# A fused transformer layer on one core: T's last quarter in another buffer, the FFN's first sums and w_down's sums at other places, and the third head's split values in buffer a

## The chip, the cores and the metric

The kernel runs on one core of a Trainium2 chip. Its engines are TensorE (PE, matmuls; PEld is its weight load), VectorE (DVE), ScalarE (ACT), GpSimd (POOL) and SyncE (SP, which here only issues transfers). Each engine works through its own queue in order; semaphores tie the queues together. The metric is the device time of one execution in microseconds, as the median of several runs.

## The reference

One layer of a hybrid encoder on x of 1024 tokens by 1024 channels: token mixing, cross-attention into 256 memory tokens, and a SwiGLU FFN, each between RMS norms and with a residual.

```python
h = rms_norm(x, mix_pre_g); proj = h @ w_in          # u | q | k | v | f_logit
y_ssm = s5_mixer(u, ...)                             # 32 groups x 16 channels, scan, gelu, GLU
y_fox = forgetting_attention(q, k, v, f_logit)       # 8 heads x 64, causal, decaying bias
x = x + rms_norm(concat(rms_norm(y_ssm), rms_norm(y_fox)) @ w_out, mix_post_g)
h = rms_norm(x, xa_pre_g)
x = x + rms_norm(memory_cross_attention(h, rms_norm(mem), wq, wkv, wo), xa_post_g)   # 4 heads x 256
h = rms_norm(x, ffn_pre_g)
x = x + rms_norm((silu(h @ w_gate) * (h @ w_up)) @ w_down, ffn_post_g)              # hidden 2816
```

## The kernel before

Every large product runs as three matmuls on operands split in a high and a low part (hi·hi, hi·lo, lo·hi; `mm3`, L122 to L124). `split` makes the parts: ACT copies the source to the high part (L113), DVE subtracts it for the low part (L115). The FFN's products (L1313) and the down projection's (L1591) have a function of their own with the same three matmuls.

The program is written as Python generators that yield between small pieces of work. A framework schedules it: it gives every buffer from a pool with a fixed number of slots, and it sets the order of each engine's queue from the program's order, from priorities (`tc.high_priority`), and from when buffers come free in its own timing of the program. So a buffer in another pool, or a call at another place, moves instructions of all engines around it. The pools that matter here are `slab` (16 large buffers), the small tags of `tt` ("a" 2, "b" 2, "c" 3, "d" 1, "e" 1, "t2" 3, which the trace calls t), `whl` (3, split weights), `raw` (2, weights as loaded), psum banks g (4) and x (4), and the FFN's `ev` (13, results of products) and `op` (10, split weights).

Three places matter.

The SSM's output. `ssm` prepares the state matrices and loads three quarters of the matrix T (made earlier and kept in `T_d`; the first quarter stays on the chip in the tile called e). `ssm_out` then has two halves s_, each of four groups b; a group is four pairs of matmuls (L647 with T, L648 with the states), summed in one psum bank, and a gelu on ACT (L649). Around it PE multiplies values: `v_tiles` makes tiles of 24 matmuls (128x256), ACT evacuates each with L318 into a t2 buffer, and POOL stores it. The split q and k tiles go through t2 and buffer a as well (L291 to L300), to `qk_d`. Buffer d holds the row `rb` that L291 multiplies by.

The out projection of the token mixing. For eight tiles of tokens j (a loop over n) PE makes two halves of 12 matmuls into x banks; DVE scales and adds (L1089), ACT squares (L1091), POOL multiplies by the gain (L1093), and DVE's L1095 to L1097 finish the row into c or e. The tiles t alternate between tags a and b. After each half `step(between)` advances `first_values`, which does matmuls of the cross-attention's values with its output weights, head by head: `value_weights(h)` loads the values of head h from `kv_d`, splits them (vh, vl), loads and splits the weights `wo`, and makes four sums of six matmuls each, which ACT and DVE evacuate. Heads 0 and 1 run inside the loop, heads 2 and 3 behind it.

The FFN. Pairs of hidden tiles are computed with seven products in place of eight (Strassen and Winograd's form): `operands` makes the sums of weights on POOL (L1416) and their splits, `gate_up` the products of a step (m is 0 for gate, 1 for up), in banks that sums are taken from: u2 is the first of them (`q.add`, DVE L1334); bank 2 is written on by a later product and has to be read first. `finish_hid` multiplies gate and up, `hid_sums` makes the four sums of the hidden tiles that the down projection's seven products want (DVE L1371), and POOL stores each to `hs_d`. `wd_sums(k)` loads a quarter of w_down's pair k // 2, makes four differences on POOL (L1386) and stores them to `wt_d` (L1387). The first pair has a start of its own and is finished by `sums(0, 1, ...)`; the loop over `seq` does the other ten pairs.

Of the kernel before, what the change touches and what calls it, by code (L numbers as in the profile page):

```python
# [9 lines left out]
F32 = mybir.dt.float32  # L10
F32R = mybir.dt.float32r
# [6 lines left out]
P = 128  # L18
# [34 lines left out]
def layer(ctx: ExitStack, tc: tile.TileContext, a, out):  # L53
# [15 lines left out]
    def slab(shape, dt=F32R):  # L69
        return slabp.tile(shape, dt, name="slab", tag="slab")  # L70
# [126 lines left out]
    def tt(tag, shape=None, dt=F32):  # L197
        return t4.tile(shape or [P, S], dt, name=tag, tag=tag, bufs=BUFS[tag])

    def t2t(shape, dt=F32):  # L200
        return tt("t2", shape, dt)
# [160 lines left out]
    def ssm():  # L362
# [20 lines left out]
        er, th, n, sn, sh, cs = cols[3:9]  # L383
# [55 lines left out]
        full = [P, NP, L, 16]  # L439
# [15 lines left out]
        for q in range(0, NP, 2):  # L455
# [4 lines left out]
            m = mi[q // 8][:, (2 * q) % 16:(2 * q) % 16 + 4, :]  # L460
# [16 lines left out]
        for b in range(8):  # L477
# [5 lines left out]
            for ri in range(2):  # L483
                for g2 in range(2):
                    o = V[ri][g2 * 64:g2 * 64 + 64, 2 * b:2 * b + 2]
                    i = ps[ri * 64:ri * 64 + 64, :, g2]
# [86 lines left out]
        tq = tt("e", [P, 8, P])  # L573
# [22 lines left out]
        for b in range(1, 4):  # L596
            n = 4 if b < 3 else 3
# [14 lines left out]
        for hf in range(2):  # L612
# [8 lines left out]
            for ri in range(2):  # L621
# [6 lines left out]
                for g2 in range(2):  # L628
                    act.activation(out=Sv[ri * 64:ri * 64 + 64, :, g2, 1:8], in_=t_[g2 * 64:g2 * 64 + 64], func=AF.Copy)
                yield  # L630
        full = [None] + [slab([P, 16, P], F32) for _ in range(2)]
        T = [[tq, full[1][:, 0:8]], [full[2][:, 0:8], full[2][:, 8:16]]]
        for hf in range(2):
            for b in range(2):
                if hf + b:
# [272 lines left out]
    with tc.high_priority(offset=boost):  # L908
# [18 lines left out]
        ws = [u_load(0)]  # L927
# [112 lines left out]
    for i in range(4):  # L1040
        hl = slab([P, 2, D])
        w = hl[:, 1].bitcast(F32)
# [4 lines left out]
    VW = {}  # L1047

    def value_weights(h):
        vh, vl = t2t([P, 2, 256], F32R), t2t([P, 2, 256], F32R)  # L1050
        vr = vl.bitcast(F32)
        sp.dma_start(out=vr, in_=kv_d[8 + 2 * h:8 + 2 * h + 2].rearrange("d p m -> p d m"))
        with tc.high_priority(offset=boost):
            split(vh, vl, vr)
        wo_ = [load_w(a["wo"][2 * h + d], 512) for d in range(2)]
        for mt in range(2):
            VW[2 * h + mt] = slab([P, 2, D])
        for c in range(2):
            tiles = [(mt, (x_ps if h == 3 else g_ps)([P, 512])) for mt in range(2)]
            for d in range(2):  # L1060
                for mt, ps in tiles:
                    ms = slice(mt * P, mt * P + P)
                    mm3(ps, vh[:, d, ms], vl[:, d, ms], wo_[d][0][:, c], wo_[d][1][:, c], d == 0, d == 1)
                    yield
            for mt, ps in tiles:
                split(VW[2 * h + mt][:, 0, c * 512:c * 512 + 512], VW[2 * h + mt][:, 1, c * 512:c * 512 + 512], ps)

    def first_values():
        for h in range(2):
            yield from value_weights(h)  # L1070

    between = first_values()
    kept = {}
# [235 lines left out]
    def product(ps, w, name, first):  # L1309
        (wh, wl), (bh, bl) = w, hB[name]  # L1310
        for k in range(4):
            for n, (x, y) in enumerate(((wh, bh), (wh, bl), (wl, bh))):
                pe.matmul(ps, x[:, k], y[:, k], start=first and k + n == 0, stop=k == 3 and n == 2,  # L1313
                          skip_group_check=not first)
# [48 lines left out]
    def hid_sums(i):  # L1363

        a11, a12, a21, a22 = hid.pop((0, 0)), hid.pop((1, 0)), hid.pop((0, 1)), hid.pop((1, 1))
        t = {}
        for name, x, y, fn in (("S3", a11, a21, ALU.subtract), ("S1", a21, a22, ALU.add),
                               ("S2", "S1", a11, ALU.subtract), ("S4", a12, "S2", ALU.subtract)):
            t[name] = ev()
            x, y = (t[v] if isinstance(v, str) else v for v in (x, y))  # L1370
            dve.tensor_tensor(out=t[name], in0=x, in1=y, op=fn)  # L1371
            hid_store(i, name, t[name])
# [55 lines left out]
        o["S1"] = op(s1)  # L1428
        return o

    def gate_up(i, m, w, q):
        q.p1(w["11"])
        p1 = q.keep(1)
        product(q.bank(4), w["S4"], "22", True)
        product(q.bank(3), w["S3"], "T3", True)
        p7 = q.keep(3)
        q.p2(w["12"])
        product(q.bank(2), w["S2"], "T2", True)
        u2 = q.add(2, p1)
        product(q.bank(3), w["22"], "T4", False)  # L1440
        product(q.bank(2), w["S1"], "T1", False)
        sums(i, m, q, p1, p7, u2, q.b[1])

    def sums(i, m, q, p1, p7, u2, c11):
        c21 = q.add(3, u2, False)
        u4 = q.add(2, p1, False)
        dve.tensor_tensor(out=p7, in0=u4, in1=p7, op=ALU.add)
        c12 = q.add(4, u4, False)
        c = {(0, 0): c11, (0, 1): c12, (1, 0): c21, (1, 1): p7}
        if m == 0:  # L1450
            for k, t in c.items():
                hid[k] = ev() if k == (0, 0) else t
                act.activation(out=hid[k], in_=t, func=AF.Silu)
        else:
            for (f, t), u in c.items():
                finish_hid(i, f, t, u)
            hid_sums(i)

    seq = [(i, m) for i in range(1, NPAIR) for m in range(2)]
    ws = {}  # L1460
# [6 lines left out]
    w = operands(0, 1, dve)  # L1467
# [15 lines left out]
    product(first.bank(3), w["22"], "T4", False)  # L1483
    product(first.bank(2), w["S1"], "T1", False)
    sums(0, 1, first, p1, p7, u2, c11)
    wd_sums(1)
    for n, (i, m) in enumerate(seq):
        if n + 1 < len(seq):
            ws[seq[n + 1]] = operands(*seq[n + 1])
        gate_up(i, m, ws.pop((i, m)), Products(i, m))  # L1490
        wd_sums(n + 2)


    fst.close()
# [168 lines left out]
```

## Time and profile before

| | before |
|---|---|
| median of 3 runs | 1402.24 us (1399.69 to 1403.91) |
| the profiled execution | 1403.55 us |
| its span, first to last instruction | 1401.8 us |
| mean granted clock of TensorE | 0.996 |
| PE busy | 1373.7 us |
| DVE, ACT, POOL busy | 973.7, 646.2, 377.3 us |
| transfers | 242.03 MB, mean 173 GB/s |

A row of a timeline reads: start, duration, engine, line, operation, result and sources, shape, count; in brackets the engine's idle time before it and what ended it. A row of the waits reads: what waited, what it waited for, total, times, longest. A row of stretches (A:B) gives busy time and count of PE, PEld, DVE, ACT and POOL, then the granted clock (1.00 is full), the share of the DMA engines and GB/s. Durations of matmuls overlap: one of 512 columns shows 0.39 us, but starts come 0.227 us apart.

### The profile page before, as it was taken

How to read it: one execution, taken by the hardware profiler on the slowest of the kernel's cores; microseconds unless marked ns; L12 is line 12 of the kernel's file. 1: busy time of each engine (PE TensorE's matmuls, PEld its weight loads, DVE VectorE, ACT ScalarE, POOL GpSimd, SP SyncE). 2: the span in 40 equal slices, each digit the busy share in tenths (PEclk: the TensorE clock that was granted, in tenths of full speed). 3: DMA queues.
4: the chain of work that ended last, by engine and by line, in shares of the span. 5: the costliest groups of instructions: out<-in, count | busy, mean ns of one | idle time of the engine just before them, and what ended most of it. 6: DMA issues, size and time to landing. Idle time of an engine off the chain costs nothing.

```text
span 1401.8 us, 19885 instructions
## 1 busy us (share of the span) xinstructions
PE 1373.7 (98%) x7149; PEld 1144.9 (82%) x7149; DVE 973.7 (69%) x1740; ACT 646.2 (46%) x1262; POOL 377.3 (27%) x430
## 2 busy tenths in 40 slices
PE   9999999999999999999999999999999999999997
PEld 7889888879978777888888778888888888888886
DVE  7959954858667678445567998787777676655566
ACT  7373345866456547433344533333333334544441
POOL 0011110001111142001111466687666651000021
PEclk9999999999999999999999999999999999999999
DMA  6435765358662865035366354555444447965544
GB/s 218 141 105 165 216 222 139 83 155 252 184 194 83 222 194 186 0 105 169 131 219 233 135 180 157 189 188 173 160 141 163 153 151 245 355 195 195 180 166 165
DMA packets 104626, 242.03 MB, mean 173 GB/s; under 512 B 11528, under 2 KB 40200, under 8 KB 104336
## 3 DMA queue, kind: packets, MB, share of 16 engines
q1 hardware_dynamic: 86000, 178.86, 40.8%
q0 software_dynamic: 18528, 61.91, 12.4%
q8 instruction: 56, 0.92, 0.3%
q14 instruction: 42, 0.34, 0.1%
HBM read 172.05 MB, written 79.43 MB: 179 GB/s over the span
## 4 chain that ended last, share of the span: by engine, by line
PE 57%; DVE 2%; issue 1%; DMA 1%; POOL 0%; ACT 0%; DVEq 0%; SPq 0%; POOLq 0%; ACTq 0%
PE x L1313 15%; PE g L1313 12%; PE x L1591 7%; PE g L1591 7%; PE g L124 2%; PE g L122 2%; PE g L123 2%; PE x L122 2%; PE x L123 2%; PE x L124 2%; PE g L1109 1%; DVE op L115 1%; PE g L1220 0%; DVE ev L1371 0%; DMA slab<-in_w_gate 0%
## 5 line engine op out<-in xcount | busy, mean ns | idle before, releaser
L1313 PE MATMUL x<-slab,op 128*128 128x512 f32 x984 | 233.4, 389 | 0.0
L1313 PEld LDWEIGHTS x<-slab,op 128*128 128x128 f32 x984 | 184.7, 188 | 38.7 <-DVE op L115 0.5
L1313 PE MATMUL g<-slab,op 128*128 128x512 f32 x756 | 182.2, 390 | 2.3 <-DVE ev L1334 2.0
L115 DVE TENSOR_TENSOR slab<-slab 128x1024 fp32r<-128x1024 f32 (+2 forms) x96 | 115.0, 1208 | 82.9 <-ACT slab L113 81.2
L1313 PEld LDWEIGHTS g<-slab,op 128*128 128x128 f32 x756 | 141.6, 188 | 32.9 <-DVE ev L1334 2.4
L122 PE MATMUL g<-slab,whl 128*128 128x512 f32 (+1 forms) x416 | 151.7, 365 | 0.8 <-ACT slab L487 0.4
L123 PE MATMUL g<-slab,whl 128*128 128x512 f32 (+1 forms) x416 | 148.4, 357 | 0.0
L124 PE MATMUL g<-slab,whl 128*128 128x512 f32 (+1 forms) x416 | 148.4, 357 | 0.0
L113 ACT ACTIVATE slab<-slab 128x1024 fp32r<-128x1024 f32 (+2 forms) x96 | 99.0, 1037 | 102.4 <-DMA slab<-hs_d 75.2
L1591 PE MATMUL g<-slab 128*128 128x512 f32 x462 | 126.6, 389 | 0.0
L1591 PE MATMUL x<-slab 128*128 128x512 f32 x462 | 126.6, 389 | 0.0
L115 DVE TENSOR_TENSOR op<-slab,op 128x512 fp32r<-128x512 f32 x82 | 99.4, 1222 | 11.9 <-ACT op L113 11.5
L1591 PEld LDWEIGHTS g<-slab 128*128 128x128 f32 x462 | 86.7, 188 | 18.0
L1591 PEld LDWEIGHTS x<-slab 128*128 128x128 f32 x462 | 86.7, 188 | 18.0
L1386 POOL TENSOR_TENSOR wt<-wt 128x256 f32<-128x256 f32 x88 | 85.7, 974 | 30.6 <-DMA wt<-in_w_down 27.3
L113 ACT ACTIVATE op<-ss 128x512 fp32r<-128x512 f32 x63 | 39.5, 629 | 106.7 <-PE g L1313 50.9
L122 PEld LDWEIGHTS g<-slab,whl 128*128 128x128 f32 x416 | 78.7, 189 | 12.2 <-ACT whl L113 0.6
L124 PEld LDWEIGHTS g<-slab,whl 128*128 128x128 f32 x416 | 78.5, 189 | 11.6 <-DVE whl L115 0.2
L123 PEld LDWEIGHTS g<-slab,whl 128*128 128x128 f32 x416 | 78.7, 189 | 10.6
L113 ACT ACTIVATE op<-slab 128x512 fp32r<-128x512 f32 x82 | 51.1, 627 | 78.4 <-PE x L1313 40.8
L115 DVE TENSOR_TENSOR whl<-raw,whl 128x1024 fp32r<-128x1024 f32 (+2 forms) x58 | 66.0, 1144 | 20.8 <-ACT whl L113 20.5
L1416 POOL TENSOR_TENSOR ss<-slab 128x512 f32<-128x512 f32 x40 | 60.8, 1520 | 62.7 <-DMA slab<-in_w_gate 22.2
(397 smaller groups left out, 2876.2 us busy)
## 6 DMA issues: line engine op xcount, KB each, us to landing
hs_d<-ev POOLq DMA_DIRECT2D x77, 256.0 KB, 2.6
slab<-hs_d SPq DMA_DIRECT2D x35, 512.0 KB, 3.9
slab<-in_w_up SPq DMA_DIRECT2D x22, 512.0 KB, 4.4
wt<-in_w_down SPq DMA_DIRECT2D x44, 256.0 KB, 3.3
wt_d<-wt POOLq DMA_DIRECT2D x22, 512.0 KB, 3.8
slab<-in_w_gate SPq DMA_DIRECT2D x20, 512.0 KB
slab<-wt_d SPq DMA_DIRECT2D x20, 512.0 KB, 8.6
wd_d<-in_w_down SPq DMA_DIRECT2D x33, 256.0 KB, 4.7
```

What stands on the lines that cost most here:

```text
L113: first = act.activation(out=hi, in_=src, func=AF.Copy, scale=1.0 if mul is None else mul)
L115: (lo_eng or dve).tensor_tensor(out=lo, in0=src, in1=hi.bitcast(F32), op=ALU.subtract)
L122: pe.matmul(ps, lh, rh, start=first, stop=False)
L123: pe.matmul(ps, lh, rl, start=False, stop=False)
L124: pe.matmul(ps, ll, rh, start=False, stop=last)
L1109: pe.transpose(tp[:, k], src[:, (k0 + k) * P:(k0 + k + 1) * P], ident)
L1313: pe.matmul(ps, x[:, k], y[:, k], start=first and k + n == 0, stop=k == 3 and n == 2, skip_group_check=not first)
L1386: pool.tensor_tensor(out=o, in0=x, in1=y, op=ALU.subtract)
L1416: made[0] = pool.tensor_tensor(out=o, in0=x, in1=y, op=fn)
L1591: pe.matmul(banks[n][j], xo[:, u, js], wo[:, v], start=ends[0] and k == 0, stop=ends[1] and k == 2, skip_group_check=onto is not None)
```

## The change

Four things are changed.

1. T's second and third quarters share one slab; the last quarter goes to buffer d. The SSM takes one slab less.
2. For the third head (h == 2) `value_weights` puts both parts of the split values in one tile of tag a in place of two t2 buffers; and `first_values` yields once more between the first two heads.
3. The four `hid_sums` of the first pair are not issued at the end of that pair, but in the first step of the second pair, behind its u2.
4. `wd_sums` runs one step later in the loop, with the last set behind the loop.

```diff
@@ ssm
-        full = [None] + [slab([P, 16, P], F32) for _ in range(2)]
-        T = [[tq, full[1][:, 0:8]], [full[2][:, 0:8], full[2][:, 8:16]]]
+        mid, tl = slab([P, 16, P], F32), tt("d", [P, 8, P])
+        T = [[tq, mid[:, 0:8]], [mid[:, 8:16], tl]]
@@ value_weights
-        vh, vl = t2t([P, 2, 256], F32R), t2t([P, 2, 256], F32R)
+        if h == 2:
+            both = tt("a", [P, 2, 2, 256], F32R)
+            vh, vl = both[:, 0], both[:, 1]
+        else:
+            vh, vl = t2t([P, 2, 256], F32R), t2t([P, 2, 256], F32R)
@@ first_values
-        for h in range(2):
-            yield from value_weights(h)
+        yield from value_weights(0)
+        yield
+        yield from value_weights(1)
@@ gate_up
-    def gate_up(i, m, w, q):
+    def gate_up(i, m, w, q, behind_u2=None):
...
         u2 = q.add(2, p1)
+        if behind_u2:
+            behind_u2()
         product(q.bank(3), w["22"], "T4", False)
@@ sums
-            hid_sums(i)
+            if i:
+                hid_sums(i)
@@ the loop
-    wd_sums(1)
     for n, (i, m) in enumerate(seq):
         if n + 1 < len(seq):
             ws[seq[n + 1]] = operands(*seq[n + 1])
-        gate_up(i, m, ws.pop((i, m)), Products(i, m))
-        wd_sums(n + 2)
+        gate_up(i, m, ws.pop((i, m)), Products(i, m), (lambda: hid_sums(0)) if n == 0 else None)
+        wd_sums(n + 1)
+    wd_sums(len(seq) + 1)
```

What this moves in the queues. First, the SSM's output on PE: g_2043 is the third group (b=2), g_2053 the fourth (b=3), g_1994 a value tile of which one matmul ran before the groups, g_2063 the next value tile. (Lines of the changed kernel are the same up to here.)

```order
 L648 MATMUL g_2043<-slab_1179,slab_1624 128x128
+L647 MATMUL g_2053<-slab_1951,slab_863 128x128
+L648 MATMUL g_2053<-slab_1179,slab_1624 128x128
...
 L123 MATMUL g_1994<-whl_1957,slab_267 128x256
 L124 MATMUL g_1994<-whl_1957,slab_271 128x256
...
 L124 MATMUL g_1994<-whl_1962,slab_274 128x256
-L647 MATMUL g_2053<-slab_1951,slab_863 128x128
-L648 MATMUL g_2053<-slab_1179,slab_1624 128x128
...
 L122 MATMUL g_2063<-whl_1957,slab_267 128x256
```

The eight rows of b=3 now stand ahead of the 23 remaining matmuls of the value tile. The same place on ACT, where L318 evacuates value tiles (g_1994 into t_2019) and L649 is the gelu of a group:

```order
 L318 ACTIVATE t_1991<-g,r_x 128x256
 L629 ACTIVATE slab<-b 64x8x112 x2
-L318 ACTIVATE t_2019<-g,r_x 128x256
 L649 ACT_TABLE_LOAD
 L649 ACTIVATE slab<-g 128x4x8x16 x4
+L318 ACTIVATE t_2019<-g,r_x 128x256
 L318 ACTIVATE t_2088<-g,r_x 128x256
```

The table load and the four gelus now stand ahead of that evacuation. On SP, the loads of T (L636) among those of q, k (L723), the decay rows nc_d and weights:

```order
-L636 DMA slab<-T_d 128x1024
-L723 DMA a<-qk_d 64x1024 x2
-L719 DMA b<-nc_d 128x1024
 L636 DMA slab<-T_d 128x1024 x2
+L723 DMA a<-qk_d 64x1024 x2
+L719 DMA b<-nc_d 128x1024
+L636 DMA d<-T_d 128x1024
 L159 DMA raw<-in_w_out_s 128x1024
```

The second load into the slab now comes with the first, ahead of the loads of q and k; the third goes to d. Second, the end of the out projection on DVE, before the change (the rows of a are those of n = 6, the rows of b those of n = 5 and then n = 7):

```order
L1089 SCALAR_TENSOR_TENSOR a<-x,r_f,a 128x512
L1097 SCALAR_TENSOR_TENSOR c<-b,r,c 128x1024
L1089 SCALAR_TENSOR_TENSOR a<-x,r_f,a 128x512
L115 TENSOR_TENSOR whl<-raw,whl 128x1024
L1095 TENSOR_REDUCE ss<-ss_5543 128x1
L139 TENSOR_SCALAR rsv<-ss 128x1
L1089 SCALAR_TENSOR_TENSOR b<-x,r_f,b 128x512
L141 SCALAR_TENSOR_TENSOR rst<-rsy,rsv 128x1
L145 SCALAR_TENSOR_TENSOR r<-rst,rsy 128x1
L1097 SCALAR_TENSOR_TENSOR c<-a,r,c 128x1024
L115 TENSOR_TENSOR slab<-g,slab 128x512
L1089 SCALAR_TENSOR_TENSOR b<-x,r_f,b 128x512
```

and after it, where five or so is added to each line number (L1094 is L1089, L1100 is L1095, L1102 is L1097):

```order
L1102 SCALAR_TENSOR_TENSOR c<-b,r,c 128x1024
L115 TENSOR_TENSOR a<-a 128x512
L115 TENSOR_TENSOR slab<-g,slab 128x512
L1094 SCALAR_TENSOR_TENSOR a<-x,r_f,a 128x512
L1100 TENSOR_REDUCE ss<-ss_5540 128x1
L139 TENSOR_SCALAR rsv<-ss 128x1
L141 SCALAR_TENSOR_TENSOR rst<-rsy,rsv 128x1
L145 SCALAR_TENSOR_TENSOR r<-rst,rsy 128x1
L1102 SCALAR_TENSOR_TENSOR c<-a,r,c 128x1024
L1094 SCALAR_TENSOR_TENSOR b<-x,r_f,b 128x512
L115 TENSOR_TENSOR whl<-raw,whl 128x1024
L1094 SCALAR_TENSOR_TENSOR b<-x,r_f,b 128x512
```

The low half of the third head's first weights (whl<-raw) stood ahead of the L1095 of n = 6 and now stands behind the last c<-a and an L1094 of n = 7; the low half of its values (a<-a) now stands early, while t<-t stood behind the last row shown of before. On PE the first product of the second head comes after one more half of the out projection, and with it all that follows of that head. Third, the FFN's start on DVE, before (L1371 the four sums, L1334 on g the u2 sum):

```order
L115 TENSOR_TENSOR op<-ss,op 128x512
L115 TENSOR_TENSOR op<-slab,op 128x512
L115 TENSOR_TENSOR op<-ss,op 128x512
L1371 TENSOR_TENSOR ev<-ev 128x512 x2
L115 TENSOR_TENSOR op<-slab,op 128x512
L1371 TENSOR_TENSOR ev<-ev 128x512 x2
L1334 TENSOR_TENSOR ev<-g,ev 128x512
L115 TENSOR_TENSOR op<-slab,op 128x512 x2
```

and after (L1376 the sums, L1339 the u2 sum):

```order
L1361 TENSOR_TENSOR ev<-ev 128x512
L115 TENSOR_TENSOR op<-slab,op 128x512
L115 TENSOR_TENSOR op<-ss,op 128x512
L115 TENSOR_TENSOR op<-slab,op 128x512 x2
L1339 TENSOR_TENSOR ev<-g,ev 128x512
L1376 TENSOR_TENSOR ev<-ev 128x512 x2
L115 TENSOR_TENSOR op<-slab,op 128x512
L1376 TENSOR_TENSOR ev<-ev 128x512
L1339 TENSOR_TENSOR ev<-x,ev 128x512
```

The u2 sum now stands ahead of the four sums and behind two more splits. On PE, ten matmuls of the next step's products, which stood ahead of the product that waits for u2 (the second one into bank 2), now stand behind it.

## The prediction

> **What bounds the kernel now.** I read the page's busy time of each engine first, then the list of what PE waits for, then the timelines and stretches around those waits.
>
> ```profile
> span 1401.8 us, 19885 instructions
> PE 1373.7 (98%) x7149; PEld 1144.9 (82%) x7149; DVE 973.7 (69%) x1740; ACT 646.2 (46%) x1262; POOL 377.3 (27%) x430
> ```
>
> PE is busy for 98% of the span, so the change can only win where PE idles or runs slowly; the number of matmuls stays the same. Where PE idles, the list of PE's waits tells (total, times, longest):
>
> ```profile
> PE g L647 <- ACT t L318: 3.2, 1, 3.2
> ...
> PE g L1313 <- DVE ev L1334: 2.0, 1, 2.0
> PE g L124 <- DVE t L115: 1.9, 2, 1.4
> ```
>
> L647 is the SSM's output, L1313 behind L1334 the FFN's start, L124 behind L115 the products with the split values: the diff touches these three places, and what I can win stands there; what I can lose is not bounded by the list.
>
> **The SSM's output (T's last quarter in buffer d).** The timeline of PE shows the end of the third group of products (b=2), 23 value matmuls, the wait, the fourth group (b=3) and a second wait; two rows of stretches give the granted clock (PEclk) around it:
>
> ```profile
> 193.55 0.39 PE L648 MATMUL g<-slab 128*128 128x128 f32 x2
> 193.69 0.36 PE L123 MATMUL g<-whl,slab 128*128 128x256 f32 x1
> ...
> 196.40 0.28 PE L124 MATMUL g<-whl,slab 128*128 128x256 f32 x1
> 199.85 0.70 PE L647 MATMUL g<-slab 128*128 128x128 f32 x2 [3.17 <-ACT t L318]
> ...
> 203.80 0.39 PE L122 MATMUL g<-whl,slab 128*128 128x256 f32 x1 [0.27 <-ACT slab L649]
> 193.70:197.00 3.30, 2.98 (x26) 2.78 (x24) 0.00 (x0) 0.00 (x0) 0.00 (x0) 1.00 0.92 322
> 200.00:203.50 3.50, 3.50 (x16) 3.24 (x16) 0.00 (x0) 1.45 (x2) 0.54 (x1) 0.52 1.03 419
> ```
>
> Between 193.69 and 203.80 PE does 23 value matmuls at about 0.12 us (2.98 us) and eight double rows which at full clock take 0.224 each (1.79 us, from the spacing of the b=2 rows). That is 4.8 us of work in 10.1 us. 3.17 + 0.27 is idle; about 1.9 us is the half clock, 0.52, that b=3 gets behind the idle stretch. Why b=3 waits, ACT, SP and POOL tell:
>
> ```profile
> 190.91 1.91 ACT L629 ACTIVATE slab<-b 64x896 f32<-64x896 f32 x2
> 199.32 0.47 ACT L318 ACTIVATE t<-g,r_x 128x256 f32<-128x256 f32 x1 [6.50 <-DMA qk_d<-t]
> 199.81 1.28 ACT L649 ACT_TABLE_LOAD   x1
> 203.15 2.07 ACT L649 ACTIVATE slab<-g 128x512 f32<-128x512 f32 x4 [2.05 <-PE g L647]
> 190.30 1.07 POOL L299 DMA_DIRECT2D qk_d<-t  x2 [6.38 <-ACT t L113]
> 184.11 0.33 SPq L636 DMA_DIRECT2D slab<-T_d  x1
> 187.54 1.14 SPq L723 DMA_DIRECT2D a<-qk_d  x2
> 190.24 0.80 SPq L636 DMA_DIRECT2D slab<-T_d  x2
> ```
>
> b=3 takes the psum bank of a value tile; that tile's evacuation (L318) needs a t2 buffer, and the store from it, issued at 190.30, lands nine microseconds later. With the change, b=3 stands ahead of the 23 value matmuls on PE, takes the bank of b=0, and needs b=0's gelu instead. ACT has the table load and the four gelus ahead of that L318. L629 ends at 192.82; table load 1.28, one gelu 2.07/4 = 0.52: 194.62. b=2 ends at about 193.75, so PE waits about 0.9 us, runs b=3 at full clock (1.79) and the 23 value matmuls (2.98) and is at the next value matmul at about 199.4 instead of 203.80. By then the other gelus are done, and the L318 that waits to 199.3 for its buffer holds only a tile that ends at the same moment. Gain 4.4 us. Bounds: 5.3 (no wait at all) and 2.5 (b=3 still at half clock). What pays: the second T load passes the two a<-qk_d loads on SP, 0.3 us of issue for them; nothing in PE's list waits for those. The last quarter in d waits for the last reader of d, DVE's L291, and then goes out where the x2 row stands now, 190.24; w_out_s and nc_d queue behind it there as before. It is read by the second half's products, some 20 us later. Cost nothing.
>
> The Trainium skill, "TensorE: Matmul & The Clock Gate", Part 1 (The HAM clock gate), says that an idle window of about 3.4 us halves the clock and a busy one restores it. The trace agrees for this place (3.17 us idle, then 0.52). By that rule a wait of 0.9 us costs no clock, as I took it.
>
> **The split values of the third head in buffer a, and a half step between the first two heads.** PE's waits there, and what ACT, DVE and SP do ahead of them:
>
> ```profile
> 536.12 0.50 PE L122 MATMUL g<-whl,t 128*128 128x512 f32 x1 [0.69 <-ACT t L113]
> 538.29 0.74 PE L124 MATMUL g<-whl,t 128*128 128x512 f32 x2 [0.51 <-DVE t L115]
> 531.02 1.05 ACT L113 ACTIVATE whl<-raw 128x1024 fp32r<-128x1024 f32 x1
> 532.10 1.53 DVE L115 TENSOR_TENSOR whl<-raw,whl 128x1024 fp32r<-128x1024 f32 x1
> 535.09 1.28 DVE L1097 SCALAR_TENSOR_TENSOR c<-a,r,c 128x1024 f32<-128x1024 f32 x1
> 536.89 0.74 DVE L1089 SCALAR_TENSOR_TENSOR b<-x,r_f,b 128x512 f32<-128x512 f32 x1
> 535.00:546.00 11.00, 8.81 (x41) 6.34 (x40) 10.69 (x17) 9.60 (x24) 3.66 (x2) 1.00 0.67 219
> ```
>
> The change gives the third head's values a free buffer early, so the waits of 0.69 and 0.51 for them go. The longer of the two waits of L124 in the list, 1.4, stays: DVE's order up to that split is unchanged and the same number of matmuls stands ahead of that lo product. But the half step delays the second head by 12 matmuls, and with its last product the release of the weight buffer that the third head's first weights want. On DVE the lo half of these weights moves from 532.10 to behind the last c<-a (535.09 to 536.3) and the next L1089 b (0.67 apart), so it ends at about 536.3 + 0.7 + 1.2 = 538.1 at the latest, and half a microsecond to a microsecond sooner, as the two 0.6 us splits that stood between them are gone: 537.5. PE comes to its first use at about 535.5 (536.12 less the 0.69 that it no longer waits): a new wait of about 2.0. Next late are the evacuations of the second head's last sums: DVE has another head's values (0.6) and another weight (1.2) ahead of them, and the third head's next product wants that bank: about 2 us more, where 0.51 and smaller waits stand now. DVE is full here, 10.69 of 11 us, so nothing is caught up. About 3.6 us of new waits less 1.2 us of old ones: a loss of 2.4 us. Bounds: a gain of 1.2 (the old waits go, none comes) and a loss of 4.4 (the load below).
>
> **The FFN's first sums.** DVE before PE's longest wait in this phase:
>
> ```profile
> 812.61 2.88 PE L1313 MATMUL x<-slab,op 128*128 128x512 f32 x12
> 825.23 3.70 PE L1313 MATMUL g<-slab,op 128*128 128x512 f32 x15 [2.00 <-DVE ev L1334]
> 818.21 2.92 DVE L1371 TENSOR_TENSOR ev<-ev 128x512 f32<-128x512 f32 x2
> 824.49 0.68 DVE L1334 TENSOR_TENSOR ev<-g,ev 128x512 f32<-128x512 f32 x1
> 825.09 3.89 DVE L115 TENSOR_TENSOR op<-slab,op 128x512 fp32r<-128x512 f32 x2
> ```
>
> The u2 sum (L1334) stands behind four L1371 sums (two such pairs) and one split. With the change two splits are ahead of it instead, one of the 3.89 pair among them: 818.21 + 0.6 + 2.1 (the larger share of the 3.89) + 0.6 = 821.5 in place of 825.1. But PE gains less, since ten matmuls of the next products now stand behind this wait and not ahead (12 take 2.72, the 2.88 of the x12 row less the 0.16 by which a last one outlasts its place, so ten take 2.3): it arrives at 825.23 - 2.00 - 2.3 = 820.9 and waits 0.6, or with a second slow split 1.5. Gain about 0.9, between the two; bounds 2.0 (the split takes 0.6, as most do) and -0.3. The four sums and their stores on POOL come later, into ring buffers that no PE row waits for.
>
> **w_down a step later** moves loads (SP), sums and stores (POOL, 27% busy). After the last step one set of sums is now done a step, 84 matmuls or 19 us, later:
>
> ```profile
> 1156.12 0.74 POOL L1387 DMA_DIRECT2D wt_d<-wt  x1 [0.30 <-POOL wt L1386]
> 1185.49 0.42 SPq L1512 DMA_DIRECT2D slab<-wt_d  x1
> ```
>
> 1156.12 + 19 is 1175, before even the first load from wt_d, and that load reads other pairs. The FFN between has no PE wait to win. Nothing, 0.3 either way.
>
> **Sum.** -4.4 + 2.4 - 0.9 = -2.9 us. Against the profiled execution (1403.55, of which 1401.8 is span) that is 1400.7; the median of the runs, 1402.24, lies 1.3 under it, so I say 1399.4.
>
> A second row of half clock has no such long wait in front of it:
>
> ```profile
> 278.35:281.76 3.41, 2.83 (x24) 2.55 (x24) 2.37 (x7) 2.76 (x8) 0.00 (x0) 1.00 0.62 153
> 281.76:285.18 3.42, 3.42 (x9) 2.66 (x9) 1.84 (x7) 2.39 (x4) 0.73 (x2) 0.52 0.53 146
> ```
>
> Half of 3.42 us, 1.7, is lost here, though PE was busy for 2.83 of the stretch before. Whether a loose stretch meets a window is chance, worth 1.7 us either way, for the new waits of the third head too. Read strictly, the Trainium skill (the page and part named above: a whole idle window) would not halve the clock after a stretch as busy as this; the row shows it, so the measurement decides.
>
> **Rivals.**
> First, the third head costs nothing and the FFN gives all: the evacuations are caught up because ACT has room (9.60 of 11 us) and the splits do not collide. Then -4.4 - 1.2 - 2.0 = -7.6, about 1394.6; with only one of the two, 1397. Against it: DVE's 10.69 of 11. With region one at its upper bound and half of these, faster: 0.3.
> Second, the change does not do what it says at the SSM: the gelu of b=0 comes as late as L318 did, since T's loads and 0.92 to 1.03 of the DMA engines' time still stand there, or the next value tile waits for the t2 buffer instead. Then only the loss of 2.4 and the gain of 0.9 are left, 1403.7, no difference to be measured. Against it: in this trace the first three groups ran without a wait, up to 193.55, and a gelu of b=0 needs no transfer.
> Third, slower: the load a<-kv_d. On SP it waits for DVE's e<-a and stands between two c<-in_x; ACT's split of it stands ahead of the next squares, which feed r for all that follows.
>
> ```profile
> t<-kv_d SPq DMA_DIRECT2D x4, 256.0 KB, 4.0
> 521.79 9.74 SPq L1082 DMA_DIRECT2D c<-in_x  x2
> 524.33 1.28 DVE L1097 SCALAR_TENSOR_TENSOR e<-a,r,e 128x1024 f32<-128x1024 f32 x1
> 528.43 0.20 ACT L138 ACTIVATE rsy<-rsy 128x1 f32<-128x1 f32 x1
> ```
>
> Issued at 525.6 with the 4.0 us of its kind it lands at 529.6, one microsecond after ACT is free for it, which DVE's work covers; each microsecond more holds ACT and DVE. Taking nine microseconds, like the store at 190.30, it lands at 534.6: 5 us of hold, -2.9 + 5 = +2.1, with a half clock behind it +3.8. It decides from about 11 us on, when the hold is past 2.9 + 4.2 = 7.1.
>
> **Chances.** 0.3% of the time, 4.2 us, is what a measurement can tell from no change. My forecast, between -4.2 and +1 of the median: 0.50; the first rival and region one's upper bound, past -4.2: 0.30; the second: 0.13; the third: 0.07, taken whole as slower. So faster 0.30, same 0.63, slower 0.07. The range, 1395 to 1404.5, reaches the first rival nearly to its end and the second. The likeliest case alone: 1398 to 1403.
>
> **What would show it.** Right: the row of L647 with a wait near 0.9 by L649, PEclk 1.00 there, PE's L122 at about 199.4; waits near 2 by DVE whl L115 and DVE slab L115 around 534; L1313's wait by L1334 between 0.5 and 1.5. Wrong: L647 still waiting for L318 or for T, the ACT row a<-a waiting for kv_d, or PE waits in the FFN by wt or ev.

## The result and the profile after

The changed kernel takes 1411.57 us in the median of 6 runs (1410.71 to 1419.51), the kernel before 1401.88 us in 6 runs beside it (1399.69 to 1404.71). The ratio is 1.0077, with a 95% interval of 1.0052 to 1.0102: about 9.7 us slower. I had forecast 1399.4 us and a range up to 1404.5. The prediction is wrong, in sign too.

The profiled execution of the changed kernel took 1411.88 us, its span 1410.1 us. From the head of its page:

```profile
PE 1376.1 (98%) x7149; PEld 1146.2 (81%) x7149; DVE 967.5 (69%) x1740; ACT 646.2 (46%) x1262; POOL 375.6 (27%) x430
```

PE does the same 7149 matmuls and is busy for 2.4 us more, which can only be slower ones; the other 5.9 us of the longer span are idle. Where, the list of PE's waits tells (total, times, longest):

```profile
PE g L1318 <- DVE ev L1339: 5.7, 1, 5.7
PE g L122 <- ACT whl L113: 2.8, 2, 2.4
PE g L123 <- DVE whl L115: 2.3, 1, 2.3
...
PE g L124 <- DVE t L115: 2.0, 1, 2.0
...
PE g L647 <- ACT slab L649: 0.8, 1, 0.8
```

The 3.2 us at L647 behind L318 are gone (the last row, now behind the gelu L649). New at the top are 5.7 us at the FFN's start and a group of waits on the operands of the second and the third head. Against the kernel before I cut the span at two instructions that both kernels have: the first L122 of `g<-e,whl` behind the SSM (444.5 us before, 436.7 after), and the first L1313 (L1318) of the FFN, `x<-slab,whl` (758.6 and 760.8).

| stretch | before | after | difference |
|---|---|---|---|
| start and SSM, to 444.5 | 444.5 | 436.7 | -7.8 |
| out projection, value weights, cross-attention, to 758.6 | 314.1 | 324.1 | +10.0 |
| FFN and down projection, to the end | 643.2 | 649.3 | +6.1 |

Of the -7.8 the SSM's change made 4.6 in this pair of executions: the lead grew from 1.2 us at 75 us, ahead of the change, to 5.8 at the first L735. The remaining two, and the 1.2, are not the change's: the half clock at 281.76 that the prediction showed is absent in this execution, and other executions of these queues have it or not.

**The SSM's output.** The wait of the fourth group on PE's timeline, and the stretch that had the half clock before (busy time and count of PE, PEld, DVE, ACT and POOL, then granted clock, share of the DMA engines and GB/s):

```profile
193.44 0.49 PE L647 MATMUL g<-slab 128*128 128x128 f32 x2 [0.75 <-ACT slab L649]
```

```profile
200.00:203.50 3.50, 3.50 (x32) 3.50 (x31) 1.28 (x2) 1.52 (x3) 0.54 (x1) 1.00 0.73 267
```

One wait of 0.75 us for the gelu, and later PE is busy for the whole 3.50 us at clock 1.00, where 0.52 stood before.

**The third head.** The load of its values on SP, ACT's split that waits for it, DVE's part of that split, and the split of the third head's weights behind it on ACT:

```profile
518.77 0.38 SPq L1056 DMA_DIRECT2D a<-kv_d  x1
530.59 0.63 ACT L113 ACTIVATE a<-a 128x512 fp32r<-128x512 f32 x1 [8.21 <-DMA a<-kv_d]
531.25 0.69 DVE L115 TENSOR_TENSOR a<-a 128x512 fp32r<-128x512 f32 x1 [6.11 <-ACT a L113]
534.86 1.04 ACT L113 ACTIVATE whl<-raw 128x1024 fp32r<-128x1024 f32 x1
```

The load lands 11.8 us after its issue (518.77 to 530.59); ACT stands for 8.21 us and DVE, whose next instruction is the low half of the same split, for 6.11; the weights' split ends at 535.9. What the transfer met, and what PE did, in stretches:

```profile
518.00:521.00 3.00, 3.00 (x15) 2.46 (x14) 2.20 (x4) 1.56 (x6) 1.04 (x2) 1.00 0.92 213
521.00:524.00 3.00, 3.00 (x15) 2.49 (x14) 2.42 (x7) 1.13 (x6) 2.04 (x2) 1.00 1.03 344
524.00:527.00 3.00, 3.00 (x15) 2.49 (x14) 1.14 (x1) 0.00 (x0) 0.00 (x0) 1.00 0.54 218
...
535.00:539.00 4.00, 0.76 (x3) 0.32 (x3) 3.88 (x6) 2.08 (x6) 0.68 (x2) 0.75 0.00 0
539.00:543.00 4.00, 4.00 (x10) 3.12 (x10) 3.35 (x6) 3.54 (x10) 2.43 (x2) 0.50 0.44 136
```

The DMA engines are full (0.92 and 1.03) when the load is issued and until 524, and half busy (0.54) until 527, with the load still under way; over its whole way, 518.8 to 530.6, their share is 0.85. In the four microseconds from 535 PE works 0.76, and after that it gets half the clock. From the first cut to the fourth head's first products (the same product at 548.6 us, 546.2 before) PE waits 11.4 us in all, against 6.3 before, and 17 products run at half clock, their starts 0.43 apart and not 0.23, which is 3.4 us: 8.5 of the 10.0.

Not all of this comes after the load's issue. A wait of the out projection, ahead of it,

```profile
502.47 0.50 PE L122 MATMUL x<-slab 128*128 128x512 f32 x1 [1.60 <-DVE a L1094]
```

0.6 us more at the L124 behind L115 (508.58) and the first of two stretches of half clock (0.50 from 509.7 to 513.0) put PE 3.5 us behind the kernel before by the last products of the second head, before it touches the third head's values.

**The FFN's first sums.** DVE, POOL and PE at the start:

```profile
819.31 4.14 DVE L1361 TENSOR_TENSOR ev<-ev 128x512 f32<-128x512 f32 x1
828.25 0.68 DVE L1339 TENSOR_TENSOR ev<-g,ev 128x512 f32<-128x512 f32 x1
819.67 1.30 POOL L1421 TENSOR_TENSOR ss<-slab 128x512 f32<-128x512 f32 x1
820.91 0.74 POOL L1391 TENSOR_TENSOR wt<-wt 128x256 f32<-128x256 f32 x1
821.61 1.28 POOL L1421 TENSOR_TENSOR slab<-slab 128x512 f32<-128x512 f32 x1
822.84 0.75 POOL L1392 DMA_DIRECT2D wt_d<-wt  x1
828.98 5.30 PE L1318 MATMUL g<-slab,op 128*128 128x512 f32 x12 [5.68 <-DVE ev L1339]
```

A product of two SBUF operands (L1361, `finish_hid`) takes 4.14 us on DVE; others of its form take 0.68 where POOL stands idle. POOL's run of two operand sums and a difference of w_down begins beside it, and the product ends 0.6 us after POOL breaks off to issue a transfer (822.84). The u2 sum comes at 828.25, and PE has waited 5.68 us for it, 3.7 more than before. The twelve products behind the wait take 5.30 us where fifteen took 3.70 before, at half clock (0.53 from 829.0 to 834.3): most of the rest of the +6.1.

### The profile page after: what moved, and what is told of

It is laid out like the page before. It is cut to its first block, busy times and chain, and to the rows that moved or that the text cites. A ratio compares the mean times of both kernels' runs of the same rounds, so it can differ in the third digit from the quotient of the medians.

```text
span 1410.1 us, 19883 instructions
## 1 busy us (share of the span) xinstructions
PE 1376.1 (98%) x7149; PEld 1146.2 (81%) x7149; DVE 967.5 (69%) x1740; ACT 646.2 (46%) x1262; POOL 375.6 (27%) x430
## 3 DMA queue, kind: packets, MB, share of 16 engines
q0 software_dynamic: 18528, 61.91, 12.1%
## 4 chain that ended last, share of the span: by engine, by line
PE 57%; DVE 2%; issue 1%; DMA 0%; POOL 0%; ACT 0%; SPq 0%; DVEq 0%; POOLq 0%
PE x L1318 15%; PE g L1318 12%; PE x L1599 7%; PE g L1599 7%; PE g L124 2%; PE g L122 2%; PE g L123 2%; PE x L123 2%; PE x L124 2%; PE x L122 2%; PE g L1114 1%; DVE op L115 1%; PE g L1225 0%; DMA wt<-in_w_down 0%; DVE ev L1361 0%
## 5 line engine op out<-in xcount | busy, mean ns | idle before, releaser
L1318 PE MATMUL x<-slab,op 128*128 128x512 f32 x984 | 233.7, 389 | 0.3 <-DVE op L115 0.3
L1318 PEld LDWEIGHTS x<-slab,op 128*128 128x128 f32 x984 | 184.6, 188 | 39.3 <-DVE op L115 0.7
L1318 PE MATMUL g<-slab,op 128*128 128x512 f32 x756 | 184.4, 393 | 5.8 <-DVE ev L1339 5.7
L1318 PEld LDWEIGHTS g<-slab,op 128*128 128x128 f32 x756 | 143.3, 190 | 36.8 <-DVE ev L1339 6.1
L115 DVE TENSOR_TENSOR slab<-slab 128x1024 fp32r<-128x1024 f32 (+2 forms) x96 | 114.7, 1207 | 83.4 <-ACT slab L113 82.1
L122 PE MATMUL g<-slab,whl 128*128 128x512 f32 (+1 forms) x416 | 151.6, 364 | 0.8 <-ACT slab L487 0.4
L124 PE MATMUL g<-slab,whl 128*128 128x512 f32 (+1 forms) x416 | 148.3, 357 | 0.0
L115 DVE TENSOR_TENSOR op<-slab,op 128x512 fp32r<-128x512 f32 x82 | 94.1, 1160 | 11.4 <-ACT op L113 11.1
L122 PEld LDWEIGHTS g<-slab,whl 128*128 128x128 f32 x416 | 78.7, 189 | 11.9 <-ACT whl L113 0.6
L113 ACT ACTIVATE op<-slab 128x512 fp32r<-128x512 f32 x82 | 51.2, 628 | 80.3 <-PE g L1318 40.3
L124 PEld LDWEIGHTS g<-slab,whl 128*128 128x128 f32 x416 | 78.5, 189 | 11.6 <-DVE whl L115 0.2
L115 DVE TENSOR_TENSOR whl<-raw,whl 128x1024 fp32r<-128x1024 f32 (+2 forms) x58 | 65.7, 1138 | 20.5 <-ACT whl L113 20.0
```

Of the source, the lines that this page charges most:

```text
L113: first = act.activation(out=hi, in_=src, func=AF.Copy, scale=1.0 if mul is None else mul)
L115: (lo_eng or dve).tensor_tensor(out=lo, in0=src, in1=hi.bitcast(F32), op=ALU.subtract)
L122: pe.matmul(ps, lh, rh, start=first, stop=False)
L124: pe.matmul(ps, ll, rh, start=False, stop=last)
```

## The experiments

Each was built from the kernel before, or from the changed kernel with a part taken out or added, and timed against the kernel before on the same chip; the chips differ from group to group. The table has the median with the number of runs, the ratio, and the three stretches of the profiled execution, cut as above, as differences to the profile before in us. The first stretch holds much chance (start, loose half clocks): the kernel before and the eight that share its SSM run the same queues up to the first cut, and their differences go from -5.6 to +3.6. The other two repeat within about 1 us. The profiled execution is one of the runs; that of "all but the third head" is the fastest of its ten, so its stretches sum to less than its median says.

| kernel | median us (n) | before | ratio, 95% | first | middle | FFN |
|---|---|---|---|---|---|---|
| T alone | 1402.63 (10) | 1402.20 | 0.9993, 0.9977 to 1.0009 | -4.3 | -0.6 | +3.7 |
| third head alone | 1413.60 (6) | 1402.20 | 1.0065, 1.0035 to 1.0096 | -0.6 | +9.1 | +3.5 |
| first sums alone | 1401.52 (10) | 1402.20 | 0.9979, 0.9961 to 0.9997 | +2.7 | -0.1 | -1.9 |
| all but the third head | 1406.26 (10) | 1402.20 | 1.0025, 1.0008 to 1.0041 | -5.6 | 0.0 | +5.2 |
| the same, POOL behind the sums | 1397.00 (9) | 1403.17 | 0.9953, 0.9938 to 0.9968 | -5.1 | -0.9 | -1.8 |
| buffer a alone | 1415.10 (4) | 1403.17 | 1.0081, 1.0049 to 1.0112 | +3.6 | +8.4 | +3.7 |
| half step alone | 1404.94 (10) | 1403.17 | 1.0020, 1.0004 to 1.0036 | -3.3 | +3.0 | +1.7 |
| third head, load on POOL's queue | 1413.50 (6) | 1403.17 | 1.0065, 1.0044 to 1.0086 | +0.8 | +6.5 | +3.5 |
| w_down alone | 1403.21 (10) | 1403.90 | 1.0001, 0.9982 to 1.0020 | -2.8 | -0.2 | +1.6 |
| all four, POOL behind the sums | 1406.37 (10) | 1403.90 | 1.0018, 0.9995 to 1.0042 | -7.1 | +9.5 | -1.8 |
| third head, split not held | 1411.14 (10) | 1403.90 | 1.0061, 1.0039 to 1.0084 | -5.6 | +6.3 | +3.6 |
| third head, fewer row loads | 1412.29 (9) | 1403.90 | 1.0067, 1.0046 to 1.0088 | -4.1 | +8.2 | +3.7 |

**T's last quarter alone.**

```diff
+        mid, tl = slab([P, 16, P], F32), tt("d", [P, 8, P])
+        T = [[tq, mid[:, 0:8]], [mid[:, 8:16], tl]]
```

> Part 1 alone (T's last quarter in d). Theory A, each part pays at its own place: the SSM place gains 4.6 us as in the changed kernel, nothing else moves by more than a half-clock stretch (1.7 us): 1396 to 1399. Rival B, the slab that is freed shifts the FFN's start too (POOL and DVE stand in another order there, which the order of this kernel shows): u2's wait grows by 2 to 4 us and the kernel stays at 1400 to 1402.

The gain at the SSM is there (PE waits 1.5 us by L649 in the place of 3.2 by L318), and the median does not move. The FFN gives 3.7 us back, though nothing of the FFN was edited. The product on DVE, POOL's run that begins beside it, and the wait on PE:

```profile
812.10 4.17 DVE L1356 TENSOR_TENSOR ev<-ev 128x512 f32<-128x512 f32 x1
812.46 1.30 POOL L1416 TENSOR_TENSOR ss<-slab 128x512 f32<-128x512 f32 x1
```

```profile
PE g L1313 <- DVE ev L1334: 2.8, 1, 2.8
```

The framework orders DVE and POOL by its own timing of the program, and the edit in the SSM changed that. In the kernel before, the two products L1356 stand together and are all but through when POOL begins (814.45), whose run there starts with a weight that has yet to land:

```profile
813.42 1.28 DVE L1356 TENSOR_TENSOR ev<-ev 128x512 f32<-128x512 f32 x2
814.45 0.85 POOL L1386 TENSOR_TENSOR wt<-wt 128x256 f32<-128x256 f32 x1 [4.16 <-DMA wt<-in_w_down]
```

With T alone the second product stands behind a split, POOL's operand sums come ahead of that weight, and the product stands still for 4.17 us.

**The third head alone** (buffer a and the half step).

> Part 2 alone (third head's split values in a, half step between the first two heads). Theory A: ACT waits some 8 us for the load a<-kv_d, PE's new waits and half-clock stretches around 500 to 550 cost 8 to 10 us: 1410 to 1412. Rival B: the load is late only because the SSM place made everything before it earlier; alone it lands in 5 us and the part costs 2 to 4 us: 1404 to 1406.

```profile
524.21 0.38 SPq L1056 DMA_DIRECT2D a<-kv_d  x1
536.53 0.63 ACT L113 ACTIVATE a<-a 128x512 fp32r<-128x512 f32 x1 [8.71 <-DMA a<-kv_d]
```

The same late landing, 12.3 us after issue, and the same middle (+9.1). By the last products of the second head it has lost 0.1 us and not 3.5, so nearly all of this +9.1 comes after them. It also has the FFN's shifted order (+3.5), as the T edit had: the same product stands for 4.17 us.

**The first sums alone** (`behind_u2`, without the others).

> Part 3 alone (the first pair's hidden sums behind the second pair's u2). Theory A: the u2 sum waits behind splits and a product of two on-chip operands that POOL holds up, PE's wait grows from 2.0 to 5 us or more with a half-clock stretch behind it: 1405 to 1408. Rival B: alone the u2 sum gains its 0.5 to 2.0 us, as predicted, and the loss comes from the order that part 1 gives POOL: 1400 to 1402.

```profile
815.81 1.28 DVE L1356 TENSOR_TENSOR ev<-ev 128x512 f32<-128x512 f32 x2
PE g L1313 <- DVE ev L1334: 0.3, 1, 0.3
```

With the two products together (1.28 for both) the FFN gains 1.9 us and the u2 wait is 0.3. In the median it is 0.0021 faster, at the limit of what can be told.

**All but the third head.** The three other parts together, to see whether the gains of T and of the first sums add up:

> Parts 1, 3 and 4, without the third head's buffer and the half step. Theory A: the 10.3 us lost around 500 to 550 come back whole and the FFN's 6.0 stay: 1411.6 - 10.3 = 1401. Rival B: a part of the loss there is only the gain of the SSM given back, because something else (the gain row's load, the x rows) sets the pace of the out projection: 1404 to 1407.

They don't: 1406.26, slower than before. The u2 wait is that of the changed kernel, and the product on DVE as well:

```profile
PE g L1313 <- DVE ev L1334: 5.7, 1, 5.7
```

```profile
811.41 4.15 DVE L1356 TENSOR_TENSOR ev<-ev 128x512 f32<-128x512 f32 x1
```

So the FFN's loss does not need the third head. The wait is longer with the sums behind u2 (5.7 us, not 2.8), though u2 comes earlier: PE goes on 68.0 us after the FFN's first product, against 69.6 with T alone. The difference is on PE, which comes 4.4 us earlier to the product that waits: fourteen products of the next step that stand ahead of it with T alone now stand behind (3.2 us), and a wait of 0.9 us on the way is gone. On DVE one split more stands ahead of u2, five where there were four.

**The same, with POOL behind the sums.** This takes POOL's run away from the products: `wd_sums(1)` and the operand sums of the third step are issued only after the store of the first of the first pair's four sums, S3.

```diff
-            ws[seq[n + 1]] = operands(*seq[n + 1])
+            with (tc.issue_after(gated[0].ins) if n == 1 else ExitStack()): ws[seq[n + 1]] = operands(*seq[n + 1])
...
-        wd_sums(n + 1)
+        with (tc.issue_after(gated[0].ins) if n == 0 else ExitStack()): wd_sums(n + 1)
```

> Parts 1, 3 and 4, and POOL's w_down sums and the operand sums of the third step are queued behind the first pair's first hidden sum, so that they stand behind u2 (DVE's order up to u2 is that of e4). Theory A, DVE's instructions on two operands in SBUF stand still while POOL works on SBUF: the product of 4.1 us takes 0.7, u2's wait falls from 5.7 to under 1 us and the kernel to 1395 to 1398. Rival B, u2 is late by DVE's own order (splits ahead of it): the wait stays over 3 us, 1401 to 1406.

```profile
809.18 0.68 DVE L1356 TENSOR_TENSOR ev<-ev 128x512 f32<-128x512 f32 x1
812.20 0.68 DVE L1334 TENSOR_TENSOR ev<-g,ev 128x512 f32<-128x512 f32 x1
813.78 0.54 POOL L1361 DMA_DIRECT2D hs_d<-ev  x1 [4.26 <-DVE ev L1371]
```

The DVE order is the one that cost 4.15 us just now, and with POOL idle from 809.5 to 813.8 each product takes 0.68. The u2 sum is out at 812.9 and PE's list has no wait of 0.4 or more in the FFN. From the start of the product to the end of u2 it takes 3.7 us here and 9.6 in the changed kernel; of the 5.9 between them the product is 3.5 and the splits behind it 2.4. The cause of the FFN's loss is shown: POOL beside DVE. At 1397.0 us, ratio 0.9953 (0.9938 to 0.9968), this is the fastest kernel of the study, faster than the kernel before and the changed one.

**Buffer a alone, and the half step alone.**

```diff
+        if h == 2:
+            both = tt("a", [P, 2, 2, 256], F32R)
+            vh, vl = both[:, 0], both[:, 1]
```

> The third head's split values in a, without the half step. Theory A, the wait of ACT for the load into a is what costs: still 6 to 11 us slower than before, ACT waits for a<-kv_d. Rival B, the half step moves that wait into the way: 1402 to 1405.

```diff
         yield from value_weights(0)
+        yield
         yield from value_weights(1)
```

> The half step between the first two heads alone, split values in t2 as before. Theory A: near before, 1401 to 1405 (the release of a weight buffer comes 2.7 us later, 2 us of new waits at most). Rival B: the half step is what costs, 1408 to 1412.

```profile
529.48 0.38 SPq L1056 DMA_DIRECT2D a<-kv_d  x1
540.47 0.63 ACT L113 ACTIVATE a<-a 128x512 fp32r<-128x512 f32 x1 [8.75 <-DMA a<-kv_d]
```

```profile
537.55 0.50 PE L122 MATMUL g<-whl,t 128*128 128x512 f32 x1 [3.27 <-ACT t L113]
```

Buffer a is nearly the whole loss (first fence, 11.0 us to landing, middle +8.4). The half step alone costs 3.0 in the middle and 0.0020 in the median (second fence): without the free buffer ACT's split of the third head's values stands behind the squares of the last row (it starts at 536.88, their end), with the load issued at 509.52 and no longer waited for.

**The third head, with the load on POOL's queue.**

```diff
-        sp.dma_start(out=vr, ...)
+        (stC if h == 2 else sp).dma_start(out=vr, ...)
```

> Part 2 with the third head's load issued by POOL in place of SP (ACT's split of it stands two squares later). Theory A, the load is late because it stands in SP's queue behind 1 MB of other loads: it lands within 5 us of its issue, ACT's wait is under 2 us, 1403 to 1406. Rival B, the transfer engines are full there whatever the queue: it lands after 9 us or more, ACT waits 5 us or more, 1409 to 1414.

```profile
524.99 0.73 POOL L1056 DMA_DIRECT2D a<-kv_d  x1
535.98 0.63 ACT L113 ACTIVATE a<-a 128x512 fp32r<-128x512 f32 x1 [5.71 <-DMA a<-kv_d]
```

Still 11.0 us. The queue that issues the load is not the cause.

**w_down alone.**

> Part 4 alone (w_down's sums a step later). Theory A: nothing waits for them, within 2 us of before. Rival B: they add to what POOL does beside DVE at the FFN's start, 1405 or more.

1.0001, as forecast. In its profiled execution the u2 wait is 2.5 and not 2.0, with a stretch of lower clock behind it, which is the +1.6; the ten runs show nothing of that.

**All four parts, with POOL behind the sums.** What is left of the whole change when the FFN is mended:

> All four parts, and POOL's sums queued behind the first hidden sum as in e5. Theory A, the FFN's loss is POOL's whatever part 2 does: u2's wait under 1 us, the FFN gives back 7 to 8 us (5.7 of wait, 1.7 of half clock): 1403 to 1405. Rival B, part 2 has its own share in the FFN's loss: 1407 or more.

```profile
PE g L122 <- ACT a L113: 3.5, 1, 3.5
PE g L123 <- DVE whl L115: 2.3, 1, 2.3
```

1406.37 us lies between the two expectations. The FFN's 7.9 us are back (+6.1 to -1.8); the middle's +9.5 is not, with the two waits shown at the head of the list. From the best kernel, which lacks only part 2, its ratio differs by 0.0065, some 9 us; the two were timed on different chips.

In the middle this kernel, the changed kernel and the third head alone have the same queues on every engine, so they repeat one experiment. By the last products of the second head PE is 1.1 us ahead of the kernel before here, 3.5 behind in the changed kernel and 0.1 behind in the third head alone; ACT gets the values 92.6, 93.9 and 92.6 us after the first cut, and the whole middle is +9.5, +10.0 and +9.1. What PE loses ahead of the values does not add: where it is early, it waits longer for the values (3.5 us here).

**The third head, split not held.** Is the loss only that ACT stands behind the split of the late values? Here the split is queued behind the root of row n = 6, so that ACT goes on:

```diff
-        with tc.high_priority(offset=boost):
+        with tc.high_priority(offset=boost), (tc.issue_after(rows_read[6].ins) if h == 2 else ExitStack()):
             split(vh, vl, vr)
```

> Part 2, but ACT's split of the third head is queued behind the root of the seventh row (n = 6) and not ahead of its squares. The load lands as late as before (11 to 12 us). Theory A, it is the hold of ACT, and of the DVE and POOL work behind it, that costs most: out of the 11 us some 5 to 8 come back, 1405 to 1409. Rival B, the late landing itself costs, as PE needs the values: 1411 to 1414.

```profile
519.39 0.38 SPq L1056 DMA_DIRECT2D a<-kv_d  x1
532.20 0.63 ACT L113 ACTIVATE a<-a 128x512 fp32r<-128x512 f32 x1 [3.43 <-DMA a<-kv_d]
532.88 0.50 PE L122 MATMUL g<-whl,a 128*128 128x512 f32 x1 [2.72 <-ACT a L113]
```

ACT waits 3.43 us and not 8.71, the middle falls from +9.1 to +6.3, and PE still waits 2.72 us for the values themselves. The edit takes only a part of the hold away, since the split of the weights still stands behind the late values on ACT, and that part is worth 2.8 of the 9.1. Of what is left, the wait for the values, 12.8 us after issue, is 2.72; waits behind DVE follow (1.33 by whl L115, 2.43 by slab L115). The two ratios (1.0061 and 1.0065) are not to be told apart.

**The third head, with fewer row loads.** To relieve the DMA engines, the x rows of the last three token tiles are not loaded (zeros by POOL instead; their residual is left out), 1.5 MB less:

```diff
-            x_read[0] = sp.dma_start(out=xt, in_=a["x"][ts, :])
+            x_read[0] = sp.dma_start(out=xt, in_=a["x"][ts, :]) if n < 5 else (pool.memset(xt, 0.0), x_read[0])[1]
```

> Part 2, with the last three rows of x not loaded (set to zero by POOL; the residual of three of eight row tiles is left out), so 1.5 MB less to transfer, 1 MB of it ahead of the third head's load. Theory A, the load is late because the transfer engines are full: it lands within 8 us in place of 12. Rival B, what makes it late is its own form (short rows) or the wait for its source: 11 to 12 us as before.

```profile
523.00:527.00 4.00, 4.00 (x19) 3.34 (x18) 3.07 (x2) 0.00 (x0) 2.73 (x3) 1.00 0.45 168
526.88 0.38 SPq L1056 DMA_DIRECT2D a<-kv_d  x1
529.93 0.63 ACT L113 ACTIVATE a<-a 128x512 fp32r<-128x512 f32 x1 [1.41 <-DMA a<-kv_d]
```

With a DMA share of 0.45 ahead of it the same load lands in 3.05 us: of the two expectations the full engines hold, and not the load's form. The time does not follow. POOL now stands behind the stores of earlier rows, since its zeros need their buffers, and with it DVE's e<-a and the load, which waits for that:

```profile
521.70 0.95 POOL L1087 MEMSET c<- 128x1024 f32 x1 [4.45 <-DMA x_d<-c]
523.93 2.92 DVE L1102 SCALAR_TENSOR_TENSOR e<-a,r,e 128x1024 f32<-128x1024 f32 x1 [3.81 <-POOL a L1098]
```

From the first cut on, the load is issued after 86.4 us, against 80.3 with the third head alone, and lands after 89.5, against 92.6. So this kernel puts a late issue in the place of most of the late landing, and its middle (+8.2 against +9.1) can't tell how much of part 2's time the landing makes; it shows only why the load lands late. That the rest of the +10.0 is the DVE order that my sum counted was only argued.

## Why the prediction was wrong

**T's last quarter: right in the mechanism, lucky in the size.** Forecast -4.4, a wait of 0.9 us by L649 and clock 1.00; measured -4.6, 0.75 and 1.00. The second rival, that the change would not do what it says here, fell. But the forecast was read from one execution. From the first L647 to the L122 that starts at 203.80 there, the nine kernels with the old SSM take 12.1 to 16.7 us (mean 14.2, in the profile before 15.4), and only five of them have the half clock, which was 1.9 of the 4.4; the five with the new SSM take 10.9 to 11.6 (mean 11.3). Over these executions, one of each kernel, the gain is 2.9 us on average.

**The third head: the step that failed is the landing of a<-kv_d.** The sum took +2.4 from DVE's order, with the load at "the 4.0 us of its kind" hidden behind DVE. It took 11.8 us, and the term is +10.0, past the loss of 4.4 that the sum gave as its bound. The mechanism stood there as the third rival, with "it decides from about 11 us on"; I gave it 0.07, because I read the landing from the median of its kind and not from the place. The rows for the place were at hand in the trace before: the loads c<-in_x beside it land in 7.8 us (median, in the list of transfers), and the stretches around the issue have the engines full:

```profile
c<-in_x SPq DMA_DIRECT2D x6, 512.0 KB, 7.8
```

```profile
520.00:524.00 4.00, 4.00 (x20) 3.30 (x19) 2.52 (x6) 1.90 (x7) 3.43 (x3) 1.00 1.00 235
524.00:529.00 5.00, 5.00 (x24) 4.14 (x23) 4.03 (x9) 2.80 (x11) 3.09 (x3) 1.00 0.89 277
```

Within that part the wait by DVE whl L115 near 2 us came as told (2.29), that by DVE slab L115 was 0.68 and not about 2. What I had at nothing, the hold of ACT ahead of its weight split, made another 2.39. And I had put a half clock behind the new waits at 1.7 us and to chance; there were two stretches, 3.4 us, of which the first comes ahead of the load. The rival's own working, with 11.8 us in the place of nine, gives 7.8 of hold and 2.4 + 7.8 = 10.2 for this part, near the 10.0 measured; that it comes so near is luck, as the waits are others. How much of the part is the landing and how much the DVE order was not separated: with the hold in part removed it is +6.3, with the load landed early but issued late +8.2.

**The first sums: right alone, wrong in company.** The term was -0.9, between -2.0 and +0.3; alone it measures -1.9, near the bound. In the changed kernel the stretch is +6.1. The step that failed is the count on DVE that put the u2 sum at 821.5: it added the durations of rows as they ran beside the old POOL order, and only for the instructions that the diff names. The order printed ahead of the prediction shows, as the first row of after, an L1361 between splits where none stood before; I gave that row no thought, and none to POOL's order. Nor is the cost the edit's own: T alone and buffer a alone each bring +3.7 here, by the order alone.

**w_down: right**, nothing.

**The sum.** Terms of single parts did not add: T alone, the first sums alone and w_down alone are 0.9993, 0.9979 and 1.0001 in the ratio, and the three together 1.0025. The first rival, faster than forecast, is what the kernel with POOL behind the sums reaches (1397.0, where the rival said 1394.6 to 1397), for two of the three reasons.

## What to carry to other kernels

Price a transfer that is moved by the share of the DMA engines at its new place, not by the median of its kind. After any edit in a program whose order a framework sets, compare the order in the stages that were not edited as well, on DVE and POOL together; a gain in one stage can be given back some 600 us later. Keep DVE's products of two SBUF operands that something waits for out of POOL's unbroken runs, by queueing POOL's work behind them where it has time.

## What the runs showed of the hardware

A DVE product of two SBUF operands stood through a whole run of POOL: 4.14 to 4.17 us in eight kernels (4.14, 4.17 and 4.15 in the three shown), over three POOL instructions each, and not through one of them. The Trainium skill, "SBUF — State Buffer", section "Who interferes with whom", says that such a product contends with a POOL instruction that reads SBUF, and in its section "Summary: rules for kernel authors" that the second to issue blocks until the first has finished. The rows agree that one blocks, but not in the order: the product starts ahead of POOL's first sum in the changed kernel (819.31 and 819.67), and even if that sum counted as the first, the product would have had its turn at 821.0, and it ended at 823.4. Elsewhere the two do take turns (two sums in 2.92 us at 818.21 before, beside POOL). What decides between the two was not tried.

This load of 256 KB took 11.0 to 13.5 us to land in the six kernels that issue it into full DMA engines (a share of 0.88 to 1.07 in the three microseconds ahead of it; 13.5 with all four parts and POOL behind the sums), from SP's queue or POOL's alike, and 3.05 us after a stretch of half that share. Why one load then gets so small a part of the engines, and why it is still under way when their mean share has fallen to 0.54, stays open.

A wait need not come near three microseconds to cost the clock. At the FFN's start the kernel before waits 2.00 us and keeps 1.00; with the half step alone it waits 2.23 and gets 0.66 behind it (the PE row, then the stretch of that kernel, then the stretch of the kernel before):

```profile
824.99 5.31 PE L1314 MATMUL g<-slab,op 128*128 128x512 f32 x15 [2.23 <-DVE ev L1335]
825.00:830.00 5.00, 5.00 (x15) 3.97 (x16) 5.00 (x5) 0.66 (x2) 3.10 (x3) 0.66 0.81 266
825.00:830.00 5.00, 4.77 (x21) 3.96 (x22) 5.00 (x5) 0.63 (x1) 3.34 (x3) 1.00 0.82 268
```

The length alone does not decide either. One and the same wait of 1.95 us, L124 behind L115, has half clock behind it in the changed kernel (0.50 from 509.7 to 513.0) and full clock with the third head alone (1.00 from 515.1 to 518.4), and a wait of 2.38 us at L647 with the half step alone keeps 1.00 (199.0 to 202.3).
